# Two transformer blocks on one core: a sixth seven-product pair in the MLP's wide down-projection, and one product of the first norm issued later

## The chip, the cores and the metric

One NeuronCore of a Trainium2 chip runs the whole program. The metric is the device time of one execution in microseconds; the kernel before takes 2393.36 us (median of 3 runs, 2393.27 to 2393.91).

## The reference

The input is one sequence of 256 tokens with 2048 channels, in float32. Two blocks follow one another. The first has a token mixer (forgetting attention and a gated recurrence behind one input projection), a convolutional feed-forward layer and a gated embedding. The second has neighbourhood attention and an MLP. The parts that the change touches are the first norm and the MLP:

```python
def rms_norm(x, g):                       # ahead of the first mixer
    xf = x.astype(jnp.float32)
    y = xf * lax.rsqrt(jnp.mean(xf * xf, axis=-1, keepdims=True) + EPS)
    return (y * g.astype(jnp.float32)).astype(x.dtype)

def sq_relu_mlp(h, w1, w2):               # h: 256 x 2048, w1: 2048 x 8192, w2: 8192 x 2048
    a = jax.nn.relu(h @ w1)
    return (a * a) @ w2
```

The kernel applies the gain g at once and the factor 1/rms per token later, since it commutes with the projections.

## The kernel before

**Weights.** All weights stream from HBM in blocks of 128 partitions by 2048 floats (1 MB). `load_parts` (L215) issues one DMA for each from the SP queue into a `raw` buffer; three such buffers exist by the time of the MLP. `pump` (L243) cuts a block into units of up to 1024 columns and splits each unit into two float32r tiles: `hi`, a rounded copy made by ScalarE (L256), and `lo`, the rest, made by VectorE (L257). In the MLP nine units can be alive; a unit's place is free once TensorE has used it. When the last unit of a block has been split, the block's buffer takes the next load.

**Products.** Each product of a weight tile with an activation tile is three matmuls that add into one PSUM bank: activation-hi with weight-hi, activation-hi with weight-lo, activation-lo with weight-hi. In `xform` (L328) these are L346, L347, L348, and 512 weight columns move past 128 tokens, for the token halves h = 0 and 1. In `wform` (L371) the weights are the stationary side (L387, L389).

**The MLP.** `MLP_PHASES` cuts the 8192 hidden channels into five phases of 12 k-tiles (1536 channels) and a last one of 4. In each of the first five phases six `wform` groups compute the squared-relu activations of two k-tiles each (`square`, L1383), `keep` stores them as hi and lo, and then the phase's part of the second product is added up: columns 0 to 1023 by `seven` (L453), columns 1024 to 2047 by two `xform` groups.

**Seven products.** `seven` takes the 12 k-tiles as six pairs. A pair is a 2 by 2 block problem: two token halves, two k-tiles, two column halves of 512. Plainly it costs eight products. For pairs named in `SEVEN` it is done with seven, in Strassen's manner as Winograd arranged it. Such a pair needs sums of activations (`sums_of`, L395: four adds and a hi and lo split of the four results, done when the activations are made) and sums of weights (`form_sums`, L232, in place in the raw buffer: L237, L240, L241), and four units in place of two: one of 512 columns and one of 1024 as loaded, then two of 1024 from the sums. The third and fourth unit wait for `form_sums`, which waits for the splits of the first two. Four accumulators `M` (kept in PSUM through all phases) and four accumulators `C` (one group each) take the products. `C[3]` takes products of plain pairs alone. As the last product into a `C` has been issued, `evac` (L1417, VectorE) adds that bank into the residual `hh`. `Sums.put` (L416) stores the activation sums: those of the first two seven-product pairs in a spare tile, the others in tiles called `S` from `room`.

**The feed-forward layer** of the first block uses the same `seven` for three phases (`w_down`), with pairs 0, 1, 3 and 4 of six, and seven units alive in place of nine.

**The first group of the mixer.** `xform(xs, 512, scaled_to(iv), pre=start)` computes with x while x is still arriving. `start` (L606) sums the squares on GpSimd, forms 1/rms per token half (`rx`), and then calls `rows_of` (L530), which spreads the 256 values of `rx` along the free axis for all partitions: two VectorE scalings of the identity (`y`, L535), two 128-column matmuls against ones (L536) and a ScalarE copy to `rrow`, followed by a scaled copy `rrowq`. `rrow` is first used after the third group; the second group (`silu_to(sg)`) needs `rx` alone.

**What sets the order.** The program is written as one stream. When it is built, a scheduler lays out each engine's queue from that stream: by order of issue, but an instruction whose inputs or buffers are late in its reckoning is passed by later ones that are ready. On the chip each queue then runs in that fixed order, and an instruction that waits holds those behind it. Queues touched here: PE, DVE (VectorE), ACT (ScalarE), and SP for the loads.

Of the kernel before, what the change touches and what calls it, by code (L numbers as in the profile page):

```python
# [8 lines left out]
F32 = mybir.dt.float32  # L9
F32R = mybir.dt.float32r  # L10
# [5 lines left out]
P = 128  # L16
T = 256
# [27 lines left out]
OUT_ORDER = list(range(6)) + list(range(8, 16)) + [6, 7]  # L45
MLP_PHASES = ((0, 12), (12, 12), (24, 12), (36, 12), (48, 12), (60, 4))

SEVEN = {"w_down": (0, 1, 3, 4), "w2": (0, 1, 3, 4, 5)}


def _groups():
# [101 lines left out]
def kernel(ctx: ExitStack, tc: tile.TileContext, x, p_t, w_in, w_out, g_mix_post, w_up, w_down,  # L153
                           g_ffn_post, w_gate, w_proj, g_ple_post, w_qkv, w_o, w1, w2, na_bias, vec, cst, lvl, out, stop=99):
# [37 lines left out]
    for name, (cols_, ks_) in _sequence(_groups()):  # L192
        bl, cn_ = _blocks(cols_, ks_)
        ent = []
        for _, n in bl:
# [3 lines left out]
            if cn_ == 1024:  # L199

                if len(ent) in SEVEN[name]:
                    new = [(b, 0, 512, False, False), (b, 1024, 1024, False, False), (b, 0, 1024, False, True), (b, 1024, 1024, True, False)]
# [125 lines left out]
    def xform(xs, cn, evac, lead=0, pre=None):  # L328


        acc = []
        for _ in range(2):
            t = mm.tile([P, 512], F32, name="acc")
            acc.append(t)
        w = Group()
        n = len(xs)
        for i in range(n + lead):
            for h, j in ((0, i), (1, i - lead)):
                if not 0 <= j < n:
                    continue  # L340
                if pre:
                    pre(h, j)
                wh, wl = w.get(j)
                xh, xl = xs[j][:, h * P:(h + 1) * P], xs[j][:, T + h * P:T + (h + 1) * P]
                o = acc[h][:, :cn]
                nc.tensor.matmul(o, xh, wh, start=(j == 0), stop=False)  # L346
                nc.tensor.matmul(o, xh, wl, start=False, stop=False)  # L347
                nc.tensor.matmul(o, xl, wh, start=False, stop=(j == n - 1))  # L348
                if j == n - 1:
                    evac(h, o)  # L350
                if h == 1:
                    w.drop(j)
                tasks.tick(cn * 1.27e-3)
# [85 lines left out]
    def shared(pool, names, M):  # L439

        o = []
        for nm in names:
            t = pool.tile([P, 2, T], F32, name=nm)
            o.append(t.rearrange("p a t -> p (a t)"))
        a, b, c, d = o
        nc.scalar.copy(a, M[0])
        nc.vector.tensor_add(d, a, M[2])
        nc.vector.tensor_add(b, d, M[1])
        nc.vector.tensor_add(c, d, M[3])
        nc.vector.tensor_add(d, c, M[1])  # L450
        return o
# [55 lines left out]
    def rstd_of(ss, n, scale):  # L507

        r = sp.tile([P, 8], F32, name="rstd", bufs=8)
        nc.scalar.activation(r[:, :n], ss, AF.Sqrt, scale=scale, bias=eps)  # L510
        nc.vector.reciprocal(r[:, :n], r[:, :n])
        return r
# [5 lines left out]
    def total(ss4):  # L518
        t = sp.tile([P, 1], F32, name="tot")
        nc.vector.reduce_sum(t, ss4, axis=AX)  # L520
        return t
# [8 lines left out]
    def rows_of(dst, r0, r1, pool, name):  # L530

        ps = aux.tile([P, 512], F32, name="ps")
        for h, r in enumerate((r0, r1)):
            d = pool.tile([P, P], F32, name=name)
            nc.vector.tensor_scalar_mul(d, ident, r)  # L535
            nc.tensor.matmul(ps[:, h * P:(h + 1) * P], ones, d, start=True, stop=True)  # L536
        nc.scalar.copy(dst, ps[:, :T])
# [19 lines left out]
    def cols(c):  # L557
        return slice(c * 512, (c + 1) * 512)
# [6 lines left out]
    for _ in range(2):  # L565
        t = xp.tile([P, D], F32, name="xt")
        xin.append(t)

    def load_x(c, hs=(0, 1)):
        for h in hs:  # L570
            nc.sync.dma_start(xin[h][:, cols(c)], x[h * P:(h + 1) * P, cols(c)])

    with tc.tile_pool(name="s1", bufs=1) as s1:
# [17 lines left out]
        for _ in range(2):  # L591
            t = s1.tile([P, H4], F32, name="QK", bufs=2)
# [13 lines left out]
        def start(h, j):  # L606
            if h == 0 and j % 4 == 0:
                for i in range(2):
                    a, b = sq[i][:, :512], sq[i][:, 512:]
                    xc = xin[i][:, cols(j // 4)]  # L610
                    nc.gpsimd.tensor_mul(b if j else a, xc, xc)
                    if j:
                        nc.gpsimd.tensor_add(a, a, b)
            if h == 0 and j == 4:
                load_x(3)
            if h == 0 and j == 9:
                lf = s1.tile([P, H4], F32, name="E", bufs=2)
                nc.sync.dma_start(cm, cst[:, K_TRI:])
                nc.sync.dma_start(vc[:, C_CW:], vec[:, C_CW:])
                nc.sync.dma_start(lf, lvl)  # L620
                nc.gpsimd.tensor_copy(lv, lf)
            if h == 0 and j < 12 and j % 2 == 0:
                enter_x(j // 2 + 2)
            if h == 0 and j == KD - 1:
                for i in range(2):
                    r = rstd_of(total(sq[i][:, :512]), 1, 1.0 / D)
                    nc.vector.tensor_copy(rx[:, i:i + 1], r[:, :1])
                rows_of(rrow, rx[:, 0:1], rx[:, 1:2], s1, "y")
                nc.scalar.mul(rrowq, rrow, 128 ** -0.5)

# [7 lines left out]
        xs = ktiles(XT)  # L638
# [275 lines left out]
        sg = s1.tile([P, 2, 512], F32, name="sg")  # L914

        def silu_to(dst):
            return lambda h, ps: nc.scalar.activation(dst[:, h, :], ps, AF.Silu, scale=rx[:, h:h + 1])
# [3 lines left out]
        warm_up(W2)  # L921
        xform(xs, 512, scaled_to(iv), pre=start)
        AT = xtiles(4)
        xform(xs, 512, silu_to(sg))
        S = s1.tile([P, H, 384], F32, name="S")
        nc.gpsimd.memset(S, 0.0)
        fg, q_, kk, cu = hgrn_tiles()
# [36 lines left out]
        S = s1.tile([P, H, 384], F32, name="S")  # L964
# [3 lines left out]
        sg = s1.tile([P, 2, 512], F32, name="sg")  # L968
# [20 lines left out]
    s2 = part.enter_context(tc.tile_pool(name="s2", bufs=2))  # L989
# [58 lines left out]
    for c in range(4):  # L1048
        gr = row(g_mix_post, c)
        def evac(h, ps, c=c, gr=gr):  # L1050
            sumsq(rp, ss[h][:, c:c + 1], ps)
            nc.vector.tensor_mul(mix[:, h, cols(c)], ps, gr)
            if c == 3:
                ts[h] = tasks.add(to_next(h, ss, C_GFFN, XN, rs))
                tasks.upto(ts[h], EARLY)
# [75 lines left out]
    for pi, (f0, fn) in enumerate(FFN_PHASES):  # L1131
        HT = xtiles(fn // 4)
        last = pi == len(FFN_PHASES) - 1
        fold = pi == len(FFN_PHASES) - 2
        S = None if last else Sums(SEVEN["w_down"], room)
        for f in range(f0, f0 + fn, 2):
            gated(f, HT, S, f0)
        if pi == 0:
            M = kept_banks()
# [234 lines left out]
    s2 = part.enter_context(tc.tile_pool(name="s4", bufs=2))  # L1374
# [8 lines left out]
    def square(f, HT, S, f0):  # L1383
        if f == 0:
            def use(i, u):
                a = s2.tile([P, 2, T], F32, name="a")
                for j in range(2):
                    nc.scalar.activation(a[:, j, :], u[j], AF.Relu)
                nc.vector.tensor_mul(a, a, a)
                keep(HT, S, 2 * i, a)  # L1390
            by_tokens(ktiles(XT), use, lambda h, i: tasks.upto(ts[h, i // 4]), lambda dst, h, ps: nc.scalar.copy(dst, ps),
                      "S", 3)
        else:
            def ev(acc):
                a = s2.tile([P, 2, T], F32, name="u")
                add_halves(s2, a, acc)
                nc.vector.scalar_tensor_tensor(a, a, 0.0, a, ALU.max, ALU.mult)
                keep(HT, S, f - f0, a)
            wform(ktiles(XT), ev)

    def room(n):
        t = s2.tile([P, 4, 256], F32R, name="S", bufs=3)
        return [t]

    for pi, (f0, fn) in enumerate(MLP_PHASES):
        HT = xtiles(fn // 4)
        last = pi == len(MLP_PHASES) - 1
        fold = pi == len(MLP_PHASES) - 2
        S = None if last else Sums(SEVEN["w2"], room)
        for f in [0] * (pi == 0) + list(range(f0 + 4 * (pi == 0), f0 + fn, 2)):  # L1410
            square(f, HT, S, f0)
        if pi == 0:
            M = kept_banks()

        def evac(h, ps, c, sub=slice(0, 512)):
            o = hh[:, h, cols(c)][:, sub]
            nc.vector.scalar_tensor_tensor(o, ps, rs[h][:, 1:2], o, ALU.mult, ALU.add)  # L1417
            if last:
                nc.sync.dma_start(out[h * P:(h + 1) * P, cols(c)][:, sub], o)

        if not last:
            seven(ktiles(HT, range(fn)), S, M, pi == 0, fold, lambda h, j, ps: evac(h, ps, j))
        if fold:
            for n, t in enumerate(shared(s2, ("a", "u", "a", "u"), M)):
                evac(n // 2, t, n % 2)
        for c in range(4) if last else (2, 3):
            if last and c == 3:
                last_product(ktiles(HT, range(fn)), lambda h, ps, sub, c=c: evac(h, ps, c, sub=sub))
            else:
                xform(ktiles(HT, range(fn)), 512, lambda h, ps, c=c: evac(h, ps, c))  # L1430
# [87 lines left out]
```

## Time and profile before

| | |
|---|---|
| median of 3 runs | 2393.36 us |
| the profiled execution's own time | 2392.92 us |
| its span, first to last instruction | 2391.1 us |
| PE / PEld busy | 2381.2 / 2019.2 us |
| DVE / ACT busy | 1759.5 / 1334.6 us |
| HBM read over the span | 447.25 MB, 188 GB/s |
| granted TensorE clock, mean | 1.000 |

PE is the matmul stream and PEld the weight loads that run beside it. The profiled execution took 0.44 us less than the median. Matmul durations overlap one another, so what a matmul takes is read from the distance between two starts. The trace names a fused tile by its program name: `hi`, `lo` and `raw` are weight units, `S` activation sums, `ps` three of the four `M` banks, `acc` the other one and the `C` banks.

### The profile page before, as it was taken

To read this page: it belongs to the slowest core of one execution; us is meant where nothing else is said; L and a number is where in the kernel's file an instruction comes from. 1 tells how busy PE (TensorE), PEld (TensorE's weight loads), DVE (VectorE), ACT (ScalarE), POOL (GpSimd) and SP (SyncE) were. 2 spreads that over 40 slices of the span, in tenths; PEclk is the share of its full clock that TensorE was granted. 3 is DMA by queue.
4 is the path that set the end of the run, shared out by engine and by line. 5 is a ranking of instruction groups with operands and counts; after the bars stand their busy time and mean duration, and the time that the engine had idled before them with its cause. 6 is when DMAs were issued, how large, how long until landed. Compare 5 with 4: busy or idle time off the path is not lost.

```text
span 2391.1 us, 31457 instructions
## 1 busy us (share of the span) xinstructions
PE 2381.2 (100%) x12265; PEld 2019.2 (84%) x12265; DVE 1759.5 (74%) x2473; ACT 1334.6 (56%) x2037; POOL 26.8 (1%) x25
## 2 busy tenths in 40 slices
PE   9999999999999999999999999999999999999999
PEld 7998888788888888888887888888888888888887
DVE  6777765688767967977786666665687877778794
ACT  5556454565555545555576566654654555545452
POOL 4000000000000000000000000000000000000000
PEclk9999999999999999999999999999999999999999
DMA  7444446454555555465554655545537364646453
GB/s 268 155 165 172 161 160 242 163 200 171 217 187 194 177 210 194 150 247 184 200 202 155 215 178 178 186 172 177 207 129 262 141 247 159 238 150 244 164 195 137
DMA packets 68966, 451.39 MB, mean 189 GB/s; under 512 B 7760, under 2 KB 8912, under 8 KB 17104
## 3 DMA queue, kind: packets, MB, share of 16 engines
q1 hardware_dynamic: 63936, 439.57, 51.2%
q10 hardware_dynamic: 4880, 9.81, 1.3%
q8 instruction: 96, 1.57, 0.3%
q14 instruction: 54, 0.44, 0.1%
HBM read 447.25 MB, written 2.10 MB: 188 GB/s over the span
## 4 chain that ended last, share of the span: by engine, by line
PE 94%; DVE 3%; ACT 1%; issue 1%; DMA 0%; POOL 0%; SPq 0%; ACTq 0%; DVEq 0%
PE acc L389 27%; PE acc L346 14%; PE acc L348 14%; PE acc L347 14%; PE acc L387 14%; DVE lo L257 2%; PE acc L490 2%; PE acc L489 2%; PE acc L491 2%; PE ps L490 1%; PE ps L491 1%; PE ps L489 1%; PE ps L659 1%; PE ps L543 1%; ACT hi L256 0%
## 5 line engine op out<-in xcount | busy, mean ns | idle before, releaser
L257 DVE TENSOR_TENSOR lo<-raw,hi 128x1024 fp32r<-128x1024 f32 (+3 forms) x917 | 1079.2, 1189 | 479.6 <-ACT hi L256 474.4
L256 ACT CAST hi<-raw 128x1024 fp32r<-128x1024 f32 (+3 forms) x917 | 921.8, 1020 | 751.1 <-PE acc L348 317.0
L389 PE MATMUL acc<-xt,hi 128*128 128x512 f32 x2816 | 874.0, 396 | 0.0
L387 PEld LDWEIGHTS acc<-xt,lo 128*128 128x128 f32 x2816 | 516.3, 188 | 116.0
L346 PE MATMUL acc<-hi,xt 128*128 128x512 f32 (+1 forms) x1528 | 592.1, 388 | 1.1 <-ACT xt L554 0.6
L348 PE MATMUL acc<-hi,xt 128*128 128x512 f32 (+1 forms) x1528 | 591.4, 388 | 0.5 <-DVE xt L555 0.5
L347 PE MATMUL acc<-lo,xt 128*128 128x512 f32 (+1 forms) x1528 | 590.6, 387 | 0.4 <-DVE lo L257 0.4
L387 PE MATMUL acc<-xt,lo 128*128 128x256 f32 x2816 | 541.5, 279 | 0.0
L389 PEld LDWEIGHTS acc<-xt,hi 128*128 128x128 f32 x2816 | 435.5, 189 | 7.2
L346 PEld LDWEIGHTS acc<-hi,xt 128*128 128x128 f32 x1528 | 287.1, 188 | 57.5 <-ACT xt L554 3.1
L348 PEld LDWEIGHTS acc<-hi,xt 128*128 128x128 f32 x1528 | 286.9, 188 | 57.4 <-DVE xt L555 2.3
L347 PEld LDWEIGHTS acc<-lo,xt 128*128 128x128 f32 x1528 | 287.4, 188 | 55.0 <-DVE lo L257 1.7
L503 ACT COPY right<-acc 128x256 f32<-128x256 f32 x176 | 57.0, 375 | 127.1 <-PE acc L389 127.1
L504 DVE TENSOR_TENSOR u<-acc,right 128x256 f32<-128x256 f32 x144 | 54.7, 419 | 45.0 <-ACT right L503 44.4
L489 PE MATMUL acc<-hi,xt 128*128 128x512 f32 x215 | 83.8, 390 | 0.4 <-ACT hi L256 0.4
L490 PE MATMUL acc<-lo,xt 128*128 128x512 f32 x215 | 84.0, 391 | 0.0
L491 PE MATMUL acc<-hi,xt 128*128 128x512 f32 x215 | 83.6, 390 | 0.0
L489 PEld LDWEIGHTS acc<-hi,xt 128*128 128x128 f32 x215 | 40.4, 188 | 9.8 <-ACT hi L256 1.5
L490 PEld LDWEIGHTS acc<-lo,xt 128*128 128x128 f32 x215 | 40.4, 188 | 9.7 <-DVE lo L257 1.1
L491 PEld LDWEIGHTS acc<-hi,xt 128*128 128x128 f32 x215 | 40.4, 188 | 8.1
L1417 DVE SCALAR_TENSOR_TENSOR hh<-acc,rstd,hh 128x512 f32<-128x512 f32 (+1 forms) x49 | 34.6, 737 | 17.1 <-PE acc L348 13.4
L237 DVE TENSOR_TENSOR raw<-raw 128x1024 f32<-128x1024 f32 x37 | 45.2, 1222 | 0.3
(343 smaller groups left out, 1684.9 us busy)
## 6 DMA issues: line engine op xcount, KB each, us to landing
raw<-in_w SPq DMA_DIRECT2D x128, 1024.0 KB, 4.8
raw<-in_w_up SPq DMA_DIRECT2D x88, 1024.0 KB, 4.8
raw<-in_w_qkv SPq DMA_DIRECT2D x48, 1024.0 KB, 4.7
raw<-in_w_in SPq DMA_DIRECT2D x46, 1024.0 KB, 4.7
raw<-in_w_down SPq DMA_DIRECT2D x44, 1024.0 KB, 4.8
raw<-in_w_out SPq DMA_DIRECT2D x16, 1024.0 KB, 4.9
raw<-in_w_gate SPq DMA_DIRECT2D x16, 1024.0 KB, 4.8
raw<-in_w_o SPq DMA_DIRECT2D x16, 1024.0 KB, 4.7
```

Source lines behind the costliest of these rows:

```text
L256: nc.scalar.copy(hi[:, j], src[:, j])
L257: nc.vector.tensor_sub(lo[:, j], src[:, j], hi[:, j].bitcast(F32))
L346: nc.tensor.matmul(o, xh, wh, start=(j == 0), stop=False)
L347: nc.tensor.matmul(o, xh, wl, start=False, stop=False)
L348: nc.tensor.matmul(o, xl, wh, start=False, stop=(j == n - 1))
L387: nc.tensor.matmul(o[:, T:], wl[:, fs[f]], x_[:, :T], start=False, stop=False)
L389: nc.tensor.matmul(o, wh[:, fs[f]], x_, start=(i == 0), stop=last)
L489: nc.tensor.matmul(o, xh, wh, start=(begin.get(id(o)) == n), stop=False)
L490: nc.tensor.matmul(o, xh, wl, start=False, stop=False)
L491: nc.tensor.matmul(o, xl, wh, start=False, stop=(end.get(id(o)) == n))
L503: nc.scalar.copy(r[:, f, :], acc[f][:, T:])
L504: nc.vector.tensor_add(dst[:, f, :], acc[f][:, :T], r[:, f, :])
```

## The change

Five edits. `SEVEN["w2"]` names all six pairs. The activations of the MLP's first group take their tile from the pool name `u` in place of `a`; the four tiles of `shared` at the last wide phase take the names `right` and `u` in place of `a` and `u`. Tiles called `S` have four buffers in place of three. In the mixer, `rows_of` and the scaled copy behind it move from the last k-tile of the first group into a new hook `second`, called at k-tile 3 of the second group.

```diff
-SEVEN = {"w_down": (0, 1, 3, 4), "w2": (0, 1, 3, 4, 5)}
+SEVEN = {"w_down": (0, 1, 3, 4), "w2": (0, 1, 2, 3, 4, 5)}
...
                     r = rstd_of(total(sq[i][:, :512]), 1, 1.0 / D)
                     nc.vector.tensor_copy(rx[:, i:i + 1], r[:, :1])
+
+        def second(h, j):
+            if h == 0 and j == 3:
                 rows_of(rrow, rx[:, 0:1], rx[:, 1:2], s1, "y")
                 nc.scalar.mul(rrowq, rrow, 128 ** -0.5)
...
-        xform(xs, 512, silu_to(sg))
+        xform(xs, 512, silu_to(sg), pre=second)
...
-                a = s2.tile([P, 2, T], F32, name="a")
+                a = s2.tile([P, 2, T], F32, name="u")
...
-                      "S", 3)
+                      "S", 4)
...
-        t = s2.tile([P, 4, 256], F32R, name="S", bufs=3)
+        t = s2.tile([P, 4, 256], F32R, name="S", bufs=4)
...
-            for n, t in enumerate(shared(s2, ("a", "u", "a", "u"), M)):
+            for n, t in enumerate(shared(s2, ("right", "u", "right", "u"), M)):
```

## Rows read from the trace of the kernel before

**Rows 1.** The page, part 1: busy time, share and count by engine.
```profile
PE 2381.2 (100%) x12265; PEld 2019.2 (84%) x12265; DVE 1759.5 (74%) x2473; ACT 1334.6 (56%) x2037; POOL 26.8 (1%) x25
```

**Rows 2.** Windows: length; busy PE, PEld, DVE, ACT, POOL; clock; DMA share; GB/s.
```profile
1988.60:1999.80 11.20, 11.20 (x66) 9.79 (x65) 6.86 (x8) 5.37 (x7) 0.00 (x0) 1.00 0.53 189
2022.20:2051.60 29.40, 29.40 (x131) 24.32 (x131) 29.20 (x37) 18.42 (x22) 0.00 (x0) 1.00 0.44 148
997.00:1027.80 30.80, 30.38 (x135) 24.77 (x133) 30.40 (x38) 19.24 (x24) 0.00 (x0) 1.00 0.46 159
```

**Rows 3.** Timeline of PE, third MLP phase: start, duration, line.
```profile
2022.27 0.39 PE L489 MATMUL acc<-hi,xt 128*128 128x512 f32 x1
...
2051.29 0.39 PE L491 MATMUL ps<-hi,S 128*128 128x512 f32 x1
...
2084.32 0.39 PE L389 MATMUL acc<-xt,hi 128*128 128x512 f32 x1
```

**Rows 4.** Timeline of DVE, same phase, wide stage; last row ACT.
```profile
2035.32 1.23 DVE L237 TENSOR_TENSOR raw<-raw 128x1024 f32<-128x1024 f32 x1
2036.45 1.23 DVE L257 TENSOR_TENSOR lo<-raw,hi 128x1024 fp32r<-128x1024 f32 x1
2037.59 0.70 DVE L240 TENSOR_TENSOR raw<-raw 128x512 f32<-128x512 f32 x1
2038.19 1.23 DVE L257 TENSOR_TENSOR lo<-raw,hi 128x1024 fp32r<-128x1024 f32 x1
2039.32 0.70 DVE L241 TENSOR_TENSOR raw<-raw 128x512 f32<-128x512 f32 x1
2039.92 0.76 DVE L1417 SCALAR_TENSOR_TENSOR hh<-acc,rstd,hh 128x512 f32<-128x512 f32 x1
2040.59 1.23 DVE L257 TENSOR_TENSOR lo<-raw,hi 128x1024 fp32r<-128x1024 f32 x1
...
2046.18 6.89 DVE L257 TENSOR_TENSOR lo<-raw,hi 128x1024 fp32r<-128x1024 f32 x6
...
2044.93 6.00 ACT L256 CAST hi<-raw 128x1024 fp32r<-128x1024 f32 x6 [3.30 <-DVE raw L237]
```

**Rows 5.** Timeline of SP: load issues. Last line: tile raw, issue to landing.
```profile
2037.71 0.33 SPq L221 DMA_DIRECT2D raw<-in_w  x1
...
2049.70 0.33 SPq L221 DMA_DIRECT2D raw<-in_w  x1
...
2309.45 0.33 SPq L221 DMA_DIRECT2D raw<-in_w  x1
...
DMA to landing us min/median/max: 4.6/5.3/6.0
```

**Rows 6.** Groups by line and shape, DVE, 2022.2 to 2051.6: busy, mean ns.
```profile
L407 DVE TENSOR_TENSOR S<-right,S 128x512 fp32r<-128x512 f32 x1 | 0.7, 690 | 0.0
L399 DVE TENSOR_TENSOR right<-u 128x128 f32<-128x128 f32 x1 | 0.3, 286 | 0.0
```

**Rows 7.** Timeline of PE, ends of the second and fifth phases' wide stages.
```profile
1921.50 0.62 PE L346 MATMUL acc<-hi,xt 128*128 128x512 f32 x2
1921.95 0.39 PE L490 MATMUL acc<-lo,xt 128*128 128x512 f32 x1
...
2311.56 0.39 PE L490 MATMUL acc<-lo,xt 128*128 128x512 f32 x1
```

**Rows 8.** Timeline of PE, third feed-forward phase: first wide matmul, next phase's first.
```profile
997.11 0.39 PE L489 MATMUL acc<-hi,xt 128*128 128x512 f32 x1
...
1060.44 0.61 PE L389 MATMUL acc<-xt,hi 128*128 128x512 f32 x2
```

**Rows 9.** Timelines of PE and DVE around the mixer's first two groups.
```profile
33.01 0.40 PE L348 MATMUL acc<-hi,xt 128*128 128x512 f32 x1
34.44 0.49 PE L536 MATMUL ps<-y,ones 128*128 128x128 f32 x2 [1.03 <-DVE y L535]
...
39.60 2.36 DVE L257 TENSOR_TENSOR lo<-raw,hi 128x1024 fp32r<-128x1024 f32 x2 [2.11 <-ACT hi L256]
```

## The prediction

> **What bounds the kernel now.** I read the busy times first: PE is busy for 2381.2 of 2391.1 us, DVE for 74% [rows 1]. So over the whole kernel only PE time counts. The change works in two places, so I read those stages next. In the wide stage of an MLP phase (window 2022.2 to 2051.6) PE is busy all 29.40 us, but DVE is busy for 29.20 of them, while in the group of `wform` before it (1988.6 to 1999.8) it is busy for 6.86 of 11.20 [rows 2]. The reader is to see that the spare DVE time that the page's 74% suggests does not exist where the change needs it. PE still has no gap there: 128 distances from the first to the last matmul of the stage, 2022.27 to 2051.29, are 0.2267 us each [rows 3], and from 2022.27 to the next phase's first matmul at 2084.32, 62.05 us, lie 129 + 144 = 273 matmuls, at 0.2267 us 61.89, so 0.16 us is lost [rows 3]. The price of a matmul here is 0.2267 us, not its duration of 0.39.
>
> The page Perfetto Trace Analysis of the Trainium skill (section "Identifying the Most-Contended Engine") holds that matmul busy time is a bad measure and weight-load busy time a good one. By it PE would have 17% to spare in this stage (24.32 of 29.40), and 15 matmuls less would be worth 15 loads of 24.32/131 = 0.186 us, 2.8 us; the even spacing leaves no such spare time, and I follow the spacing.
>
> **The pair, on PE.** Pair 2 costs seven products in place of eight, in five phases: 5 x 3 matmuls x 0.2267 = 3.40 us less. All of it is on the path.
>
> **The pair, on DVE.** Its two units become four: one split of 512 and one of 1024 columns more, and three weight sums. By distances of starts a split of 1024 takes 1.14 (2036.45 to 2037.59), L237 1.13 (2035.32 to 2036.45), L240 0.60 (2037.59 to 2038.19), L241 0.60 (2039.32 to 2039.92) [rows 4]; the split of 512 I take like L240, of the same size, at 0.60. Together 4.07 us. What goes: with pair 2 changed no product enters `C[3]`, so its `evac` at 2039.92 falls away, 0.67 us to the next start [rows 4]. Net 3.40 us more DVE work per stage, in a stage where DVE has 0.2 us of rest. It cannot be done ahead: the units' places are freed by the stage's own matmuls. The activation sums of pair 2, four instructions of 0.29 and one of 0.69 [rows 6], 1.8 us, come in a `wform` group with 4.3 us of DVE rest [rows 2]: I cost them at nothing. ACT's two casts and one copy more find 11 us of rest in the stage [rows 2], also nothing.
>
> How late is the last unit then? In the third phase the last split of the last pair has ended when its raw buffer is loaded again, at 2049.70 [rows 5]. The first matmul with that `lo` is the fifth from the stage's end, 2051.29 - 4 x 0.2267 = 2050.38 [rows 3]: 0.68 us of room. In the fifth phase the same two are 2309.45 [rows 5] and 2311.56 [rows 7]: 2.11 of room. With the change the split ends 3.40 us later and PE wants it 0.68 us earlier, 4.08 in all, so 2.0 to 3.4 us are missing per phase.
>
> **What fills the gap.** These are not lost one for one, since the order of PE's queue is made at build time and lets ready matmuls pass. It does so already: in the second phase two matmuls of the next group (L346) stand ahead of the stage's last four, at 1921.50, and PE goes on at 1921.95 without a gap [rows 7]. So I follow the third phase with everything 3.40 us later on DVE. PE reaches the third unit of the last pair at 2051.29 - 11 x 0.2267 - 0.68 = 2048.1. Its `hi` cast starts at 2044.93 and takes 1.0 (six in 6.00 us), its `lo` split starts at 2046.18 [rows 4]; with 3.40 they are at 2048.3 and 2049.6, the `hi` done at 2049.3. What else is there at 2048.1? `C[3]`'s bank is never used, so the next group's first half can start in it, with `hi` alone. Its weights' load is issued at 2037.71 and takes 5.3 [rows 5], later by 3.40: landed 2046.4, two casts done by 2048.5. Four k-tiles, two matmuls each that need no `lo`, are 8 x 0.2267 = 1.8 us: PE is covered to 2049.9, when the late `hi` is there (four matmuls, to 2050.8), and the late `lo` has ended at 2050.8 (2046.18 + 3.40 + 1.23). So the cover nearly holds, with under a microsecond in doubt at each of three places: the casts, the `lo`, and the `evac` of a `C` bank before the second half can start. The nearest stage with a DVE as full is the third feed-forward phase (30.40 of 30.80 us [rows 2]): from 997.11 to 1060.44 lie 132 + 144 = 276 matmuls, 62.57 us, and it took 63.33 [rows 8], so it loses 0.76. Against the 0.16 of now I charge 0.5 us per phase, 2.5 us in five. Bounds: 0 if the cover is whole, 2.0 to 3.4 per phase if nothing covers. After the stage a unit of 1024 columns gives PE 12 matmuls, 2.72 us, for 1.14 us of DVE, so a backlog of 3.40 is gone after two or three units and nothing is carried on.
>
> **The other tile names.** `u` for the first group's activations and `right` in `shared` put a wait on tiles last read in the same queue before; a fourth `S` buffer only gives room. Nothing, either way.
>
> **The spread product.** PE's last matmul before it starts at 33.01, the product at 34.44, held by `y` on DVE [rows 9]: 1.43 less 0.23, 1.20 us lost. In the second group `rx` is long there, and DVE rests 2.11 us before 39.60 [rows 9], about where k-tile 3 is, so the two scalings are in time. The two matmuls are still paid; two DVE and two ACT instructions move with them, no DMA and no wait on SP or POOL. What is late next? PE comes 1.2 us earlier into a group whose weights are ready ahead (DVE itself waits, so the buffers are full of finished splits). I take all 1.20; bounds 0 and 1.20.
>
> **Sum.** -3.40 + 2.5 - 1.20 = -2.1 us. The profiled execution took 2392.92, so 2390.8; the median lies 0.44 higher: 2391.3 us, 0.09% below before.
>
> **The rivals.**
> (1) DVE's lateness is paid in full. PE runs its queue in order, and the place is the first matmul with the third unit of pair 5: if the built order leaves it in front, everything behind waits. For it: DVE is full; in the third phase no such passing is seen, the stage ends with its own matmuls [rows 3]. Against: the passing in the second phase [rows 7]. Price: 4.08 less a room of 0.68 to 2.11, 2.7 in the middle, times five is 13.4; with -3.40 and -1.20 +8.8, so 2402.2 us. It decides once the scheduler reckons those splits in time when they are not. The page TensorE: Matmul & The Clock Gate of the Trainium skill ("Step-by-step: what each phase is for") says that matmuls stay in program order and only weight loads are pulled ahead: the chip by itself would not pass the late matmul, and no row here shows it doing so.
> (2) The cover starts too late: the next group's `hi` casts stand behind the late ones in ACT's queue. Then PE rests from 2048.1 to 2049.3 in each phase, 1.2 us, beside the 0.5: 5 x 1.7 - 4.6 = +3.9, 2397.3 us. For it: only casts already landed can pass, and the load is just in time.
> (3) The cover is whole and the mixer's wait is gone: -4.6, 2388.8 us. Against it: the feed-forward stages, each with some loss.
> (4) The mixer's edit does nothing, because the wait goes to the next matmul: +1.2 on any case, inside their ranges.
>
> **Chances.** Forecast 0.60, its own range 2389.5 to 2394; rival 1 0.15; rival 2 0.15; rival 3 0.10. A measurement of this kernel tells 0.2%, 4.8 us, from no change. Faster by more, below 2388.6, needs rival 3 and something beyond it, half of it at most: 0.05. Slower by more, above 2398.15: rival 1 and a third of rival 2, together 0.20. The rest, 0.75, is within. The range of 2388.5 to 2399 leaves out rival 1 and the ends of the others, under 0.2.
>
> **What would show it.** Right: 126 in place of 129 matmuls in each wide stage, DVE full to its end, no `evac` from a fourth bank, L346 and L348 standing among the stage's last matmuls in all five phases, each phase 0.2 us shorter than now, no wait of PE at L536. Wrong: a wait of PE for `hi` or `lo` of more than a microsecond before L489 or L490 at the end of a stage, five times; or the 1.2 us turning up again at the start of the second group.

## The result and the profile after

The kernel after takes 2412.81 us (median of 6 runs, 2411.85 to 2413.69), the one before, timed beside it, 2393.46 (6 runs, 2393.15 to 2393.91): 19.35 us more, ratio 1.0080 with an interval of 1.0070 to 1.0091. The forecast was 2391.3, its range ended at 2399.0; rival 1, paid in full, had been priced at 2402.2. The profiled execution of after took 2413.66 us, one of the two longest of the six; its span is 2411.9, 20.8 above before. Of all executions in this document one, of the kernel with the plain pair last, ran in a slower state (2602.42 us at a granted clock of 0.85); it moves the median of that kernel's 11 by 0.02 us and has no part in its ratio.

The page's first part, to set beside [rows 1]:

```profile
PE 2391.3 (99%) x12250; PEld 2017.0 (84%) x12250; DVE 1782.4 (74%) x2518; ACT 1345.8 (56%) x2052; POOL 26.6 (1%) x25
```

PE has the 15 matmuls less that were counted, and DVE 45 instructions more: per phase a pair's two splits and three sums, its four adds and one split of activations, less the one `evac`. Yet PE is not the sum of its matmuls any more. Starts of the first wide matmul and of the next phase's first matmul, for the first two phases:

```profile
1763.71 0.39 PE L489 MATMUL acc<-hi,xt 128*128 128x512 f32 x1
...
1828.53 0.39 PE L389 MATMUL acc<-xt,hi 128*128 128x512 f32 x1
...
1895.51 0.39 PE L489 MATMUL acc<-hi,xt 128*128 128x512 f32 x1
...
1963.52 0.39 PE L389 MATMUL acc<-xt,hi 128*128 128x512 f32 x1
```

Between the two starts of a phase lie 270 matmuls now, 61.21 us at 0.2267 each, and before 273, 61.89 us. What a phase takes beyond that is called lost here (the same two starts are read in every phase and in every kernel below, from the one profiled execution of each):

| lost, us | 1st phase | 2nd | 3rd | 4th | 5th | sum |
|---|---|---|---|---|---|---|
| before | 0.28 | 0.24 | 0.17 | 0.50 | 0.49 | 1.7 |
| after | 3.61 | 6.80 | 6.78 | 3.60 | 5.34 | 26.1 |

So 24.4 us more are lost. With 3.40 of matmuls saved that is +21.0, and the first phase begins 0.3 earlier than before (1763.71 against 1764.00): +20.7 of the span's +20.8. The mixer's gain shows less in this one execution than in the medians below; the wait for the input, the L600 below, took 0.4 more in it than in the profile of before (0.9). Where the time is lost, the waits of PE show (us in total, times, longest):

```profile
PE ps L489 <- ACT hi L256: 4.7, 5, 1.3
PE acc L489 <- ACT hi L256: 4.4, 7, 1.0
PE ps L600 <- DMA xt<-in_x: 1.3, 2, 0.8
PE ps L490 <- DVE lo L257: 1.1, 2, 0.5
...
PE acc L490 <- DVE lo L257: 0.9, 3, 0.4
PE acc L346 <- ACT hi L256: 0.9, 4, 0.2
```

The wait of 1.03 for `y` before L536 [rows 9] is gone, and L489 now waits for `hi`. The waits for `hi` and `lo` in this list come to 12.0 us, less than half of the 26.1 lost, because a wait costs more than its length: before 1793.74, in the rows further down, PE waits 0.56, but the two starts lie 0.95 apart (1792.79 and 1793.74) and the next one 0.34 on, 0.84 more than twice 0.2267. Distances up to a matmul's duration of 0.39 show no wait at all, and a part of the loss is the clock (last section).

The five wide stages, each from its first matmul to its last, to set beside the second row of [rows 2]; the last line is the first phase's stage before:

```profile
1763.60:1796.30 32.70, 31.13 (x131) 23.49 (x130) 32.41 (x42) 18.59 (x23) 0.00 (x0) 1.00 0.38 133
1895.40:1930.40 35.00, 32.35 (x130) 24.50 (x129) 34.86 (x44) 20.00 (x24) 0.00 (x0) 0.93 0.36 125
2030.40:2066.20 35.80, 33.05 (x135) 24.59 (x134) 34.44 (x43) 19.99 (x24) 0.00 (x0) 0.99 0.37 130
2165.40:2198.00 32.60, 30.99 (x130) 23.38 (x129) 32.30 (x42) 18.52 (x23) 0.00 (x0) 1.00 0.37 131
2297.20:2331.50 34.30, 31.09 (x130) 23.24 (x129) 34.15 (x44) 20.59 (x25) 0.00 (x0) 1.00 0.37 125
...
1764.00:1793.40 29.40, 29.40 (x131) 24.04 (x129) 29.14 (x38) 18.26 (x22) 0.00 (x0) 1.00 0.44 148
```

DVE is busy to within 0.3 us of the whole stage in four of five, while PE rests 1.6 to 3.2 us. The stage has changed its bound: it lasts as long as DVE's work. In the first and fourth phases that work is 32.4 us, in the first the 29.1 of before and the 3.40 that the prediction added, less 0.1. In the others it is 2 us more, in stages that are 2 to 3 us longer. The groups of DVE in the first and the second of these stages tell what:

```profile
L257 DVE TENSOR_TENSOR lo<-raw,hi 128x1024 fp32r<-128x1024 f32 x15 | 18.0, 1219 | 1.2 <-ACT hi L256 1.2
...
L257 DVE TENSOR_TENSOR lo<-raw,hi 128x1024 fp32r<-128x1024 f32 x17 | 20.2, 1218 | 1.2 <-ACT hi L256 1.2
```

Two splits more, and the wide stage itself has the same in both, so they are work of the next group. Where they stand in DVE's queue the ends of the stages show. The third and fifth phases have 17 as well.

The end of the first phase's stage, DVE, ACT and PE in turn:

```profile
1790.11 0.68 DVE L240 TENSOR_TENSOR raw<-raw 128x512 f32<-128x512 f32 x1
1790.71 1.22 DVE L257 TENSOR_TENSOR lo<-raw,hi 128x1024 fp32r<-128x1024 f32 x1
1791.85 0.68 DVE L241 TENSOR_TENSOR raw<-raw 128x512 f32<-128x512 f32 x1
1792.45 1.40 DVE L1420 SCALAR_TENSOR_TENSOR hh<-acc,rstd,hh 128x512 f32<-128x512 f32 x2
1793.77 3.48 DVE L257 TENSOR_TENSOR lo<-raw,hi 128x1024 fp32r<-128x1024 f32 x3
...
1792.64 4.84 ACT L256 CAST hi<-raw 128x1024 fp32r<-128x1024 f32 x5 [2.45 <-DVE raw L241]
...
1790.24 0.50 PE L489 MATMUL ps<-hi,S 128*128 128x512 f32 x1 [0.67 <-ACT hi L256]
...
1792.79 0.39 PE L491 MATMUL ps<-hi,S 128*128 128x512 f32 x1
1793.74 0.50 PE L489 MATMUL acc<-hi,xt 128*128 128x512 f32 x1 [0.56 <-ACT hi L256]
...
1794.69 0.73 PE L346 MATMUL acc<-hi,xt 128*128 128x512 f32 x2 [0.21 <-ACT hi L256]
1795.26 0.39 PE L490 MATMUL acc<-lo,xt 128*128 128x512 f32 x1
```

The last unit needs sum, cast and split one behind the other: L241 from 1791.85, the cast from 1792.64, the split from 1793.77. ACT rested 2.45 us before that cast although casts of the next group stood behind it: five run in a row as soon as it may go, and the load of the first of them had been issued at 1780.99, where a load takes 5.3 us [rows 5]. So the next group's `hi` came after the late one, and two L346 were all the cover that PE had. The fourth phase ends in the same order.

The end of the second phase's stage, PE, then ACT and DVE:

```profile
1923.34 0.73 PE L489 MATMUL ps<-hi,S 128*128 128x512 f32 x2 [1.33 <-ACT hi L256]
1924.60 0.50 PE L490 MATMUL ps<-lo,S 128*128 128x512 f32 x1 [0.53 <-DVE lo L257]
...
1926.78 0.80 PE L489 MATMUL acc<-hi,xt 128*128 128x512 f32 x1 [0.79 <-ACT hi L256]
...
1927.80 1.15 PE L346 MATMUL acc<-hi,xt 128*128 128x512 f32 x2
...
1922.25 1.99 ACT L256 CAST hi<-raw 128x1024 fp32r<-128x1024 f32 x2 [3.24 <-DVE raw L237]
1924.73 3.89 ACT L256 CAST hi<-raw 128x1024 fp32r<-128x1024 f32 x4 [0.49 <-DMA raw<-in_w]
...
1924.47 0.69 DVE L241 TENSOR_TENSOR raw<-raw 128x512 f32<-128x512 f32 x1
1925.07 5.76 DVE L257 TENSOR_TENSOR lo<-raw,hi 128x1024 fp32r<-128x1024 f32 x5
```

Here it is the other way about. The last unit's sum, L241, ends at 1925.16, so no cast that began before is the late one. Of the two from 1922.25 the first waited for L237 and is the third unit's; the second, and the first of the four from 1924.73, which waited for a load, belong to the next group. At 0.97 us each the first of the four ends at 1925.7 and the second at 1926.7, which is when PE's wait ends: the late cast stood second, half a microsecond after its sum was ready. DVE likewise had begun two splits of the next group, at 1925.07 and 1926.2, before the late cast ended; the late split came third, 0.6 us after its cast. The fifth phase ends in the same order. In the third phase the late cast is the third of four from 2060.04, the first of them after a load: PE's wait of 1.05 ends at 2063.03, as the third is done, and two splits stand ahead of the late one there too. Seven matmuls of the next group pass in it (the first at 2057.94), and PE rests all the same.

The product of the first norm, in the mixer's second group:

```profile
38.53 0.39 PE L536 MATMUL ps<-y,ones 128*128 128x128 f32 x2
...
39.29 0.49 PE L536 MATMUL ps<-y,ones 128*128 128x128 f32 x2
```

No wait of PE stands before either.

### The profile page after: what moved, and what is told of

It reads as the page before. It is cut to its first block, busy times and chain, and to the rows that moved or that the text cites. A ratio compares the mean times of both kernels' runs of the same rounds, so it can differ in the third digit from the quotient of the medians.

```text
span 2411.9 us, 31493 instructions
## 1 busy us (share of the span) xinstructions
PE 2391.3 (99%) x12250; PEld 2017.0 (84%) x12250; DVE 1782.4 (74%) x2518; ACT 1345.8 (56%) x2052; POOL 26.6 (1%) x25
## 4 chain that ended last, share of the span: by engine, by line
PE 92%; DVE 5%; ACT 1%; issue 1%; DMA 1%; SPq 0%; ACTq 0%
PE acc L389 27%; PE acc L346 14%; PE acc L348 14%; PE acc L347 14%; PE acc L387 13%; DVE lo L257 3%; PE acc L490 1%; PE acc L489 1%; PE acc L491 1%; ACT hi L256 1%; DVE raw L237 1%; PE ps L662 1%; PE ps L490 1%; PE ps L491 1%; PE ps L543 1%
## 5 line engine op out<-in xcount | busy, mean ns | idle before, releaser
L346 PE MATMUL acc<-hi,xt 128*128 128x512 f32 (+1 forms) x1528 | 593.1, 389 | 1.6 <-ACT hi L256 0.9
L346 PEld LDWEIGHTS acc<-hi,xt 128*128 128x128 f32 x1528 | 287.4, 188 | 59.7 <-ACT xt L554 3.1
L348 PEld LDWEIGHTS acc<-hi,xt 128*128 128x128 f32 x1528 | 287.4, 188 | 57.4 <-DVE xt L555 2.3
L489 PE MATMUL acc<-hi,xt 128*128 128x512 f32 x190 | 75.4, 399 | 4.5 <-ACT hi L256 4.4
L490 PE MATMUL acc<-lo,xt 128*128 128x512 f32 x190 | 74.7, 396 | 0.9 <-DVE lo L257 0.9
L491 PE MATMUL acc<-hi,xt 128*128 128x512 f32 x190 | 74.2, 391 | 0.0
L237 DVE TENSOR_TENSOR raw<-raw 128x1024 f32<-128x1024 f32 x42 | 51.2, 1218 | 0.2
L489 PEld LDWEIGHTS acc<-hi,xt 128*128 128x128 f32 x190 | 35.7, 188 | 17.7 <-ACT hi L256 10.8
L490 PEld LDWEIGHTS acc<-lo,xt 128*128 128x128 f32 x190 | 35.8, 188 | 10.9 <-DVE lo L257 3.4
L554 ACT ACTIVATE xt<-ps,vc 128x128 fp32r<-128x128 f32 x128 | 41.8, 367 | 5.0 <-DVE xt L555 3.2
```

The lines of the kernel that those rows point to most:

```text
L237: nc.vector.tensor_sub(r[:, :1024].rearrange("p (a c) -> p a c", a=2), r.rearrange("p (a b c) -> p a b c", a=2, b=2)[:, :, 1, :], r[:, :10 ...
L489: nc.tensor.matmul(o, xh, wh, start=(begin.get(id(o)) == n), stop=False)
L491: nc.tensor.matmul(o, xl, wh, start=False, stop=(end.get(id(o)) == n))
```

## The experiments

Each kernel is timed beside the kernel before (medians 2393.95, 2393.76 and 2393.82 in three groups of experiments, 21 to 25 runs each). The letters of the theories are each expectation's own; what follows is said in words.

**The spread product alone, twice, and with the tile names.** The first and last kernels move `rows_of` into `second` and nothing else; the middle one adds all edits but the pair (tile names, fourth `S` buffer).

```diff
+        def second(h, j):
+            if h == 0 and j == 3:
...
-        xform(xs, 512, silu_to(sg))
+        xform(xs, 512, silu_to(sg), pre=second)
```

> The kernel before with the spread product moved to the second group, and nothing else. Theory A (the mixer's part is a small gain, the whole loss is the pair's): PE's rest of 1.2 us at 34.4 is gone, minus the rest of 0.3 us that the changed kernel shows at its L536: -0.9 us, 2392.5. Theory B (the moved step costs something later, since the changed kernel had only 0.3 us of the 1.2 left at the MLP's first wide stage): between -0.3 and +1 us.

> The changed kernel with five pairs again, so that the tile names, the fourth S buffer and the spread product are all that is left of the change. Theory A: as the spread alone, -1.5 us. Theory F (the names u and right add waits): between -1 and +4 us.

> The spread product's move alone, once more, to narrow its interval: 1.2 to 1.5 us below the kernel before, ratio 0.9994 to 0.9995, as in the first look; 0.3 above to 0.3 below if that was chance.

Measured: 2392.45 (11 runs), 0.9994 [0.9986, 1.0003]; 2392.51 (10 runs), 0.9993 [0.9984, 1.0003]; 2392.19 (11 runs), 0.9992 [0.9983, 1.0001]. That is -1.50, -1.25 and -1.63 us, with 1.70 us lost in the MLP as before. Each interval takes in no change, though all three fall on the same side and all runs of the third (to 2393.15) lie below all runs of before beside it (from 2393.47). The traces say more than the medians: the MLP's first wide matmul starts between 1763.14 and 1763.71 us in all seven profiled kernels with the move, and between 1764.00 and 1765.63 in all five without. The first expectation took off 0.3 for a rest at L536 that is none for PE (above). The names and the buffer cost nothing that shows.

**The pair without the spread product.** The diff of the change less the two hunks above.

> The changed kernel without the moved spread product. Theory A: +20 us against before, 2413 to 2414, all of it inside the five wide stages of the MLP and their xform groups. Theory B: clearly less than the changed kernel's +19.4, by 1 us or more, since the moved step would have had a part in it.

Measured 2414.50 (4 runs), +20.55, ratio 1.0085 [1.0072, 1.0099]; 26.25 us lost, as in after. The pair makes the whole loss, as theory A had it, and with the change's +19.35 the spread product is worth -1.2 here too.

**Nothing but DVE later.** The kernel before, with three further splits of pair 2's two units that write the same `lo` again.

```diff
+                    if name == "w2" and len(ent) == 2:
+                        more.update({len(units): 3, len(units) + 1: 2})
...
-                nc.vector.tensor_sub(lo[:, j], src[:, j], hi[:, j].bitcast(F32))
+                for _ in range(more.get(state["u"], 1)):
+                    nc.vector.tensor_sub(lo[:, j], src[:, j], hi[:, j].bitcast(F32))
```

> The kernel before, five pairs with seven products, with three further splits of 1024 columns on DVE for pair 2 (the same lo written again), 3.4 us per stage: DVE's extra work alone, no change in matmuls, units or places. Theory A: the loss appears without the pair, 3.4 less the room of 0.7 to 2.1 us per stage and more where the order suffers: +8 to +18 us. Theory C: under +3 us.

Measured 2405.23 (4 runs), +11.3, ratio 1.0050 [1.0034, 1.0065]; 13.05 us lost, so 11.4 more than before, for 5 x 3.42 = 17.1 us of DVE work. The same waits appear, with PE's program unchanged in its products. Fourth phase:

```profile
2187.36 0.73 PE L493 MATMUL ps<-hi,S 128*128 128x512 f32 x2 [1.65 <-ACT hi L259]
2188.62 0.50 PE L494 MATMUL ps<-lo,S 128*128 128x512 f32 x1 [0.53 <-DVE lo L261]
...
2190.66 0.50 PE L493 MATMUL acc<-hi,xt 128*128 128x512 f32 x1 [0.85 <-ACT hi L259]
```

DVE's lateness alone makes these rests; neither the seven products nor new tiles are needed. What it costs is uneven, though: the five phases lose 1.35, 2.49, 2.80, 4.44 and 0.27 us more than before, for the same 3.42 of work in each.

**One further split.** As above, with one in place of three (1.14 us per stage).

```diff
+                        more.update({len(units): 2})
```

> As the kernel with three further splits for pair 2, with one: 1.14 us of DVE work per stage in place of 3.4. Theory A: the room of 0.7 to 2.1 us per stage takes up nearly all of it: 0 to +1.5 us against before, where three cost +11.3. If the loss is in proportion to the DVE work instead, +3.8 us.

Measured 2395.80 (10 runs), +2.0, ratio 1.0009 [0.9999, 1.0018]; 3.75 us lost, 2.05 more than before. That lies between the two forecasts, and the interval just takes in no change.

**The pair without its weight sums.** The kernel after, with `form_sums` left out for pair 2; its matmuls, casts and splits stay.

```diff
+                    if name == "w2" and len(ent) == 2:
+                        formed.add(b)
```

> The changed kernel with the weight sums of pair 2 left out (its third and fourth unit are split from the raw weights; part of the result is not that of the reference), so that matmuls, units, splits and loads are all as in the changed kernel and only 2.33 us of DVE work per stage are gone. Theory A (DVE is late and PE's fixed queue waits): DVE has 1.07 us more than before in place of 3.40, with 0.68 less time: most of the loss goes, -2 to +4 us against before. Theory C (four units hold the raw buffer and the places longer, so that loads and casts come late): the sums matter little, +12 to +20 us.

Measured 2394.03 (10 runs), +0.1, ratio 1.0000 [0.9991, 1.0009]; 6.48 us lost. Taking 2.33 us of sums per stage away from DVE gives back 19.7 of the 26.1 lost, so theory C falls. The splits that remain still cost more than the pair saves (4.8 against 3.40); the kernel is level with before because it keeps the spread product's gain.

**One pair fewer.** The kernel before with pairs 0, 1, 3 and 5.

```diff
+SEVEN = {"w_down": (0, 1, 3, 4), "w2": (0, 1, 3, 5)}
```

> The kernel before with four of six pairs (0, 1, 3, 5) done with seven products: PE has 3.4 us more, DVE 3.4 us less per stage. Theory A (a stage loses only where DVE is late): the five stages lose nothing, so +3.4 less at most 1.4 us of today's losses: +2 to +3.4 us. Theory D (the losses come from seven-product pairs as such, through their longer chains from sum to cast to split): the step from five to six cost 20, so the step from four to five should cost as well, and this kernel is faster than before.

Measured 2395.75 (10 runs), +2.0, ratio 1.0009 [0.9999, 1.0018]. Nothing is lost in the MLP (0.04 us in five phases); the fifteen matmuls more cost 3.40 and 1.65 come back. That is theory A's lower end, and theory D falls. In the third phase's stage DVE now rests 2.7 us of 29.9:

```profile
2024.00:2053.90 29.90, 29.90 (x133) 24.78 (x132) 27.20 (x34) 18.64 (x22) 0.00 (x0) 1.00 0.58 211
```

**A sum on GpSimd.** The kernel after, with the last sum of every wide pair (L241) on GpSimd.

```diff
-            nc.vector.tensor_sub(r[:, 1024:1536], r[:, 1024:1536], r[:, 1536:])
+            (nc.gpsimd if b in wide2 else nc.vector).tensor_sub(r[:, 1024:1536], r[:, 1024:1536], r[:, 1536:])
```

> The changed kernel with the last weight sum (L241) of every w2 pair on GpSimd in place of VectorE: 0.6 us x 6 less DVE work per stage, so DVE has about what it has before. Theory A alone: the loss goes, -4 to +2 us against before. Theory E (GpSimd slows DVE beside it: in the start of the kernel before a split of 1024 took 2.31 us beside a GpSimd product, 1.22 without): each sum on GpSimd costs DVE about 1 us and saves 0.6, so the loss stays or grows: +15 to +35 us.

Measured 2423.48 (4 runs), +29.7, ratio 1.0124 [1.0109, 1.0139]; 36.6 us lost. Of GpSimd's groups over the span, then DVE's from 2035 to 2060, one timeline row of PE, and a window:

```profile
L244 POOL TENSOR_TENSOR raw<-raw 128x512 f32<-128x512 f32 x30 | 62.9, 2096 | 2093.2 <-DVE raw L243 2040.6 <-ACT S L409 43.6 <-ACT hi L259 9.0
...
L260 DVE TENSOR_TENSOR lo<-raw,hi 128x1024 fp32r<-128x1024 f32 x9 | 12.9, 1429 | 5.3 <-ACT hi L259 5.3
...
2054.65 0.50 PE L492 MATMUL acc<-hi,xt 128*128 128x512 f32 x1 [1.40 <-ACT hi L259]
...
2056.60:2060.00 3.40, 3.40 (x10) 2.69 (x9) 2.90 (x3) 1.79 (x2) 1.27 (x1) 0.53 0.84 308
```

DVE has six sums less per phase, 30 x 0.69 = 20.7 us in all, and the kernel is 10 us slower than after. Theory A falls. The loss is in theory E's range, but not by its price: DVE's busy time in all is 1775.8 us, 6.6 less than in after, so some 14 of the 20.7 went to slower work beside GpSimd (of the nine splits above two took 2.23 and 2.12 us, the others 1.22) and DVE still came out ahead. What grew is the chain: the sum takes 2.10 us in place of 0.69, the unit's cast and split stand behind it, and DVE waits 5.3 us for casts in 25. The clock has a share too: it fell to half for 3.4 us in four phases, as in the last line, with some eight matmuls at 0.43 us each time, 1.6 us. So about 6.4 of the 36.6 lost are the clock's, against 3.3 in after. How much of the rest is the longer chain and how much the slower splits, this run does not tell apart.

**The plain pair last.** Five pairs, 0 to 4, and the spread product moved.

```diff
+SEVEN = {"w_down": (0, 1, 3, 4), "w2": (0, 1, 2, 3, 4)}
```

> Five seven-product pairs as before, with the plain pair last (0 to 4 named, 5 plain) and the spread product moved. DVE's work per wide stage is that of the kernel before; only its order differs. Theory A (the lateness is paid where a stage's last units hang on a weight sum: sum, cast, split one behind the other): the last two units now need no sum, so the 1.70 us that the five stages of before lose go to 0.3 or less, and with the spread's 1.2 the kernel comes out 2.5 to 3 us below before. Theory F (only the amount of DVE work in a stage counts, wherever the sums stand): lost time stays at about 1.7, the kernel 1.2 to 1.5 below before. Against both: C[3]'s bank is now added into the residual at the very end of a stage, ahead of the next group's splits, which could put 0.2 to 0.7 us per phase back.

Measured 2393.61 (11 runs), -0.2, ratio 0.9999 [0.9990, 1.0008]; 3.01 us lost, not 0.3 and not 1.7. Both theories fail. The stage's end is now free of waits as the first had it, but PE rests in the middle instead, in the fifth phase here:

```profile
2302.20 0.39 PE L489 MATMUL ps<-hi,S 128*128 128x512 f32 x1
2302.76 0.50 PE L490 MATMUL ps<-lo,S 128*128 128x512 f32 x1 [0.17 <-DVE lo L257]
```

The plain pair gives PE 24 matmuls (5.4 us) for two splits (2.3 us); at place 2 it would let DVE come back level before the last pairs, which is argued and not shown. By the time lost order counts, and the place that the kernel had is the better one; the medians cannot tell the two kernels apart.

**The loss against the extra DVE time.** DVE's time is per stage; lost is the sum of five phases, from one profiled execution each.

| DVE us beyond before | kernel | lost |
|---|---|---|
| -3.40 | four pairs | 0.04 |
| 0 | before | 1.7 |
| 1.14 | one further split | 3.75 |
| 1.07 + 0.68 | pair without sums | 6.48 |
| 3.42 | three further splits | 13.05 |
| 3.40 + 0.68 | after | 26.1 |

The 0.68 is the three matmuls less, by which PE comes sooner. The first 1.1 us cost 0.4 per stage; the last step, from 3.42 to 4.08, costs 2.6, and that step is not only one of amount: in after the added work is also a chain, and the clock (last section) has a share of 0.7 in it. The sums hide how uneven the phases are (0.27 to 4.44 with three further splits).

## Why the prediction was wrong

**Right.** The saving on PE: 15 matmuls, 3.40 us. DVE's work: 3.40 us per stage forecast, 3.3 by the busy time of the first phase (32.41 against 29.14), and the `evac` of the fourth bank is gone. The spread product: 1.20 forecast, 1.2 to 1.6 by four differences of medians. The tile names: nothing.

**Wrong: the step "What fills the gap".** It set the 4.08 us of lateness against matmuls of the next group and charged 0.5 us per phase, 2.5 in all. The runs showed 24.4. The step counted PE's matmuls that need no `lo` and asked when their weights land; it did not ask in which order ACT and DVE would take them. It assumed that the next group's two casts, and none of its splits, were done by the time that PE arrives. In the first and fourth phases the next group's casts stand behind the late one; in the second, third and fifth, casts of the next group stand ahead of it, and two splits with them. Behind, the cover is not there: two matmuls pass in place of eight. Ahead, the late unit is later for it, and only in the third phase does PE's own order make use of the cover (seven matmuls). The first case is rival 2's condition, the second its reverse. The prediction's own sign of being wrong, a wait of over a microsecond at a stage's end, came in three phases; in the other two the waits are 0.67 and 0.56. The traces show the order, and the run with DVE alone later shows that lateness suffices. That a better order would have covered it was not tried, and the queues' order was not changed by itself in any run.

**The size**, from after's phases:
- DVE's lateness: the first and fourth phases, where the late unit goes first and the clock holds, lose 3.33 and 3.10 more than before, 3.22 in the mean. That is rival 1's 4.08 less a room of 0.9, inside the 0.68 to 2.11 that it read (it had 2.7). Five times 3.22 is 16.1.
- The order: the fifth phase loses 4.85 more, 1.63 above that; in three phases 4.9. Set beside the first phase alone, by the distances of PE's starts, it loses 0.96 more at the last unit, behind the two splits of the next group, 1.12 more at the third unit, whose sum L237 (2322.68) stands behind an `evac` (2322.02) there and ahead of both in the first phase, and 0.34 less before. So the two splits are not the whole of it.
- The clock, below: the second phase loses 6.56 more, 1.7 above the fifth, whose rests are alike; the third has some eight matmuls at a spacing of 0.43 in place of 0.2267, 1.6. Together 3.3.

16.1 + 4.9 + 3.3 = 24.3 of the 24.4. Two of the three terms are differences between phases, so the sum comes out by the way it is made and is no test. The first term in particular is a reading of two phases: with DVE alone later, 3.42 us cost 0.27 to 4.44. Rival 1 was the right mechanism: its price of 13.4 stands near the first term only, the clock was in no rival, and the order only in the form of rival 2. Its condition, that the scheduler reckons the late splits in time when they are not, fits the order of the queues in after and is no more than argued: no run shows what the scheduler reckoned.

The Trainium skill, page TensorE: Matmul & The Clock Gate ("Step-by-step: what each phase is for"), has matmuls in program order. The trace does not contradict it: at 1795.26 the L490 follow only behind the L346 that waited 0.21 for its `hi`. It cannot show it either, since no row tells whether a matmul that was ready stood behind a waiting one.

**The weak reading** was that of the room. The feed-forward stage that loses 0.76 with a DVE as full [rows 2, 8] was taken as the nearest row, and its loss for an upper mark of the price. But a stage in which DVE is full and on time says nothing of one in which DVE has 3.4 us too much: before, the MLP stage already lost 0.34 per phase (the run with four pairs loses none), so it stood at the edge and every further microsecond had to be paid or hidden. The order, too, could have been read: of the six splits from 2046.18 [rows 4] the last unit's is the third, which ends as its buffer is loaded again at 2049.70 [rows 5], so a split of the next group stood ahead of it even then.

The best version found is the kernel before with the spread product moved: 1.5 and 1.6 us below it, less than one comparison can tell from none.

## What to carry to other kernels

When a change moves work from PE to another engine, read the windows of the stage it lands in: if that engine is busy to the end there, count on its added time becoming the stage's, however free it is elsewhere; phase by phase it may cost nothing or more than its length. Work of the next stage covers such a gap only if it stands well in every queue on its way, casts and splits too; ahead of the late piece it makes it later, behind it it comes too late. And where a chain (sum, cast, split) stands at a stage's end, look at the time of each piece before moving one to an idle engine: here the slower engine made the kernel 10 us longer, though the busy one had less to do.

## What the runs showed of the hardware

TensorE's granted clock fell to 0.50, which is 1.2 GHz, after short rests. Windows of after: the rests of the second phase, the stretch behind them and the next; the third phase's; and the fifth's:

```profile
1918.30:1925.40 7.10, 5.24 (x22) 3.55 (x21) 7.06 (x10) 3.37 (x5) 0.00 (x0) 1.00 0.54 193
1925.50:1932.20 6.70, 5.91 (x15) 3.82 (x14) 5.99 (x6) 3.12 (x4) 0.00 (x0) 0.50 0.40 136
1932.40:1939.20 6.80, 6.80 (x31) 5.63 (x31) 3.31 (x3) 4.00 (x4) 0.00 (x0) 1.00 0.92 331
2065.50:2068.80 3.30, 3.30 (x10) 2.48 (x9) 2.36 (x4) 0.00 (x0) 0.00 (x0) 0.50 0.97 410
2320.00:2331.50 11.50, 8.29 (x32) 4.92 (x30) 11.46 (x14) 7.23 (x9) 0.00 (x0) 1.00 0.38 125
```

The clock was half for 6.8 us in the second phase and for 3.4 in the third, and matmul starts lay 0.43 us apart there. Before the first fall PE had rested for 1.33 and 0.53 us (waits at 1923.34 and 1924.60). The fifth phase has nearly the same rests and kept the full clock, and so did the fourth phase of the kernel with DVE alone later, with waits of 1.65, 0.53 and 0.85:

```profile
2186.00:2193.00 7.00, 4.04 (x14) 2.24 (x14) 6.46 (x8) 5.43 (x6) 0.00 (x0) 1.00 0.26 111
```

So the same rests bring the fall in one place and not in another, and in one execution and not in another: the four executions of the kernel with DVE alone later show mean clocks of 1.000, 0.999, 1.000 and 0.998, and the last is the longest (2407.06 us against 2405.01 to 2405.39). The six of after show 0.997 to 0.999, and the two at 0.999 are the shortest (2412.20 and 2411.85). What decides was not found. A GpSimd subtraction of 128x512 took 2.10 us in the mean of 30 where DVE takes 0.69, and DVE's splits took 1.43 us in the mean of the stretch with it where they take 1.22.
